# Where a norm scale is multiplied in, and which engines split weights into a rounded part and a rest, in a two-layer encoder step

## The chip, the cores and the metric

The program runs on one core of a Trainium2 chip. The metric is the device time of one execution in microseconds (us). The time before is the median of three timed runs. The core has five engines that run their own instruction lists in order and wait for each other through semaphores: TensorE (PE in the profile, its weight loads PEld), VectorE (DVE), ScalarE (ACT), GpSimd (POOL), and SyncE (SP), which issues the DMAs.

## The reference, cut to what matters

Each of two layers normalises its input, projects it to 13 groups of columns, runs four kinds of attention on them, and projects back. The parts that the change touches:

```python
def rms(x, g):
    xf = x.astype(jnp.float32)
    y = xf * lax.rsqrt(jnp.mean(xf * xf, -1, keepdims=True) + EPS)
    return (y * g.astype(jnp.float32)).astype(x.dtype)

xn = rms(x, lp['norm_g'])                       # (2048 + 64 rows) x 1024
aq, ak, av, ag, bcq, ... = split_in(xn @ lp['w_in'])
k, v = jnp.split(rms(mem, lp['m_norm_g']) @ lp['w_mem_kv'], 2, axis=-1)
y = rms(heads(y, N_OUT_HEADS), lp['out_g'].reshape(N_OUT_HEADS, HEAD_DIM))
y = y.reshape(x.shape[:2] + (MIX_WIDTH,)) * jax.nn.silu(gates)
return x + y @ lp['w_out']
```

In all three projections a gain `g` per input feature stands between the normalised activations and the weights. Since `(x * g) @ W` and `x @ (g * W)` (row k of W scaled by g of feature k) are the same product, the gain can be multiplied into either side. The factor per row of `rms`, the rsqrt, is applied at the end, when a product leaves PSUM.

## The kernel before, in words

Projections run in a three-product form: both sides are split into a part rounded to the matmul's type (`h`, float32r) and the rest (`l`), and a product is `xh*wh + xh*wl + xl*wh`. In the code `xh`, `xl` are the transposed activations of one tile of 128 rows (8 k tiles of 128 features each) and `wh` is one buffer that holds the rounded weights and, behind them, the rest.

The rows are split into three blocks (6, 6 and 5 tiles; the last tile is the 64 sample rows). A *job* is one projection of one block: `i` is the input projection (13 *chunks* of at most 256 output columns), `o` the output projection (4 chunks), `m` the memory's keys and values (2 chunks, 2 tiles). The jobs run in the order `i00 m00 i01 i02 o00 m10 o01 i10 i11 o02 i12 o10 o11 o12` (layer, block), 106 chunks in all. Within a chunk the loop runs over the tiles of the block, and within a tile over the 8 k tiles.

- `prep` makes a tile's `xh` and `xl`, in two halves of four k tiles: TensorE transposes (L259), ScalarE copies the half from PSUM with rounding (L266, 512 columns), VectorE subtracts (`sub_r`, L136, 512 columns). This happens once per tile and job, one tile ahead of the products in the first chunk of a job, or during the last chunk of the job before.
- `weights` makes one chunk's weights: four DMAs of two k tiles each into `raw`, then for each k tile GpSimd multiplies by the gain column and rounds (L304, `gc[:, k:k+1]`), and VectorE computes `raw * gain - h` (L305). There are 8 buffers `wh`, one per k tile, which is one chunk's worth: the k tile of the next chunk can only be written when the last tile of this chunk has used the old one. So all of a chunk's splitting happens around the *boundary* between two chunks, and the next chunk's first tile follows at once.
- `p_stream` runs the jobs and interleaves `feed` (the next weights) with the products (L402, L403, L405; for the narrow chunk of 160 columns L400 and L405). `pp` (PSUM, two buffers) is evicted by ScalarE (`ev`, L437).
- `attention` runs beside it: scores, a maximum or a scan on VectorE, exponentials or sigmoids on ScalarE, transposes, the split `ph` (L903 on ScalarE, L136 on VectorE), and the product with the values (L925). In group C (`Stick`) VectorE scans (L1110) and GpSimd multiplies (L1113).

The program's text gives the order in which work is generated; a scheduler then fixes the order of the instructions on every engine from its own model of durations.

Of the kernel before, what the change touches and what calls it, by code (L numbers as in the profile page):

```python
# [7 lines left out]
F32 = mybir.dt.float32  # L8
F32R = mybir.dt.float32r
BF16 = mybir.dt.bfloat16  # L10
ACTF = mybir.ActivationFunctionType
# [53 lines left out]
def hybrid_step(  # L65
# [12 lines left out]
    SAMP = NT  # L78
# [157 lines left out]
        if left[tag] == 0:  # L236
            done.add(tag)

    def prep(load, norm, acts, t, split):

        xs = []
        for q in range(2):
            xs.append(pj.tile([128, 512], F32, tag="xin", name="xin", bufs=2))
            load(xs[q], q)
        yield 0
        xh = pj.tile([128, 8, 128], F32R, tag="xh", name="xh", bufs=MAXB)
        xl = pj.tile([128, 8, 128], F32R, tag="xl", name="xl", bufs=MAXB)
        st = None
        if norm:
            st = pj.tile([128, 4], F32, tag="xst", name="xst", bufs=MAXB + 1)  # L250
        acts[t] = (xh, xl, st)
        for q in range(2):
            x = xs[q]
            if norm:
                A.activation(out=xl[:, q * 4:q * 4 + 4].rearrange("p a b -> p (a b)"), in_=x, func=ACTF.Square,
                             accum_out=st[:, q:q + 1])
            pt = ps_st.tile([128, 4, 128], F32, name="ptx")
            for k in range(4):
                T.transpose(pt[:, k, :], x[:, k * 128:(k + 1) * 128], ident)  # L259
            ks = slice(q * 4, q * 4 + 4)  # L260
            if t == SAMP and split:
                A.copy(out=xl[:, ks], in_=pt)
                copy_r(xh[:, ks, 0:64], xl[:, ks, 0:64].bitcast(F32))
                sub_r(xh[:, ks, 64:128], pt[:, :, 64:128], xl[:, ks, 64:128])
            else:
                A.copy(out=xh[:, ks], in_=pt)  # L266
                sub_r(xl[:, ks], pt, xh[:, ks])
            yield 1024
        if norm:
            V.tensor_tensor(out=st[:, 2:3], in0=st[:, 0:1], in1=st[:, 1:2], op=ALU.add)  # L270
            V.tensor_scalar(out=st[:, 2:3], in0=st[:, 2:3], scalar1=1.0 / 1024, scalar2=EPS,
                            op0=ALU.mult, op1=ALU.add)
            rpow(st[:, 3:4], st[:, 2:3], 1)
# [22 lines left out]

    def weights(job, c0, w, out):

        gc = job.gcols()

        def split(raw, k):
            hl = pj.tile([128, 512], F32R, tag="wh", name="wh", bufs=8)
            h, lo = hl[:, 0:w], hl[:, w:2 * w]
            G.tensor_scalar(out=h, in0=raw, scalar1=gc[:, k:k + 1], scalar2=1.0, op0=ALU.mult, op1=ALU.mult)  # L304
            V.scalar_tensor_tensor(out=lo, in0=raw, scalar=gc[:, k:k + 1],  # L305
                                   in1=h.bitcast(F32), op0=ALU.mult, op1=ALU.subtract)
            out.append((hl[:, 0:2 * w], h, lo))

        n = 2
        src = job.wsrc[:, 8 * c0:8 * (c0 + w)].rearrange("p (k c) -> p k c", k=8)  # L310
        raws = []
        for k in range(0, 8, n):
# [2 lines left out]
            raws.append(raw)  # L315
            yield 0
            if k > 0:
                for i in range(n):
                    split(raws[-2][:, i, 0:w], k - n + i)
                    yield 0  # L320
        for i in range(n):
            if i:
                yield 0
            split(raws[-1][:, i, 0:w], 8 - n + i)

    def p_stream(jobs):
        chunks = [(j,) + c for j in jobs for c in j.chunks]
# [32 lines left out]
        def start_prep(j, t):  # L360

            if (j, t) not in ready:
                ready.add((j, t))
                begin(j)
                preps[j, t] = prep(j.loader(t), j.norm, j.acts, t, j.folds(t))
                next(preps[j, t])

        def prep_tile(j, t):
# [1202 lines left out]
```

## Time and profile before

| | |
|---|---|
| median of three runs | 3382.83 us (3377.99 to 3388.35) |
| profiled execution | 3392.03 us, span 3390.2 us |
[...]
| PE busy | 94% of the span, 24486 matmuls |
| DVE busy | 80%, 7976 instructions |
| ACT busy | 57%, 5336 instructions |
| POOL busy | 47%, 2353 instructions |

The three pointwise engines are not equally loaded: VectorE is busy for four fifths of the span, ScalarE and GpSimd for about half of it. A matmul of 256 columns is shown at about 290 ns although the next one starts long before its end, so idle time of PE is shorter than what a wait costs. A row of the waits says which engine waited for whose instruction, for how long in all, how many times, and how long the longest took.

### The profile page before, as it was taken

Reading aid. Unit: us, or ns where it says so; the run is one execution under the profiler, and the core shown is the slowest. Engines: PE = TensorE matmul, PEld = TensorE weight load, DVE = VectorE, ACT = ScalarE, POOL = GpSimd, SP = SyncE. Lnnn points to the kernel's source line nnn. Section 1 sums busy time; section 2 is a strip of 40 time slices with the busy share of each in tenths; the row PEclk is TensorE's granted clock in tenths of the full one; section 3 lists DMA queues with packets and bytes.
Section 4 is the critical chain, followed back from the end, with each engine's and each line's share of the span. In section 5 each row is a group of like instructions: output and inputs, shape, how many; then the busy total and the mean of one; then the engine's idle time right before and its main releaser. Section 6 shows DMA issues by size and latency. Waiting matters only on the chain. (4 is left out here: it accounts for less than half of the span.)

```text
span 3390.2 us, 75857 instructions
## 1 busy us (share of the span) xinstructions
PE 3177.9 (94%) x24486; PEld 3029.8 (89%) x24486; DVE 2728.9 (80%) x7976; ACT 1939.0 (57%) x5336; POOL 1598.4 (47%) x2353
## 2 busy tenths in 40 slices
PE   8999899899999998999999899988999999999898
PEld 7899899789999988999999788978898998888898
DVE  5686777999788789887778977899878888776994
ACT  4455655567665555566556665656646566654651
POOL 4564455666344256542434635477424454112563
PEclk9999999999999998999999999999999999999999
DMA  6555776435656656565566567634455766556534
GB/s 198 168 147 165 205 203 191 131 101 155 172 155 192 194 165 166 141 191 154 145 186 193 146 177 209 194 111 118 140 142 160 207 193 192 151 149 179 153 110 147
DMA packets 576123, 558.95 MB, mean 165 GB/s; under 512 B 70960, under 2 KB 478000, under 8 KB 575728
## 3 DMA queue, kind: packets, MB, share of 16 engines
q1 hardware_dynamic: 575728, 554.10, 58.3%
q8 instruction: 196, 3.21, 0.4%
q14 instruction: 199, 1.63, 0.2%
HBM read 378.21 MB, written 173.75 MB: 163 GB/s over the span
## 5 line engine op out<-in xcount | busy, mean ns | idle before, releaser
L403 PE MATMUL pp<-wh,xh 128*128 128x256 f32 x4416 | 1268.4, 291 | 33.6 <-DVE wh L305 32.3
L402 PE MATMUL pp<-wh,xh 128*128 128x256 f32 x4416 | 1259.8, 290 | 21.9 <-ACT ev L437 14.4
L405 PE MATMUL pp<-wh,xl 128*128 128x256 f32 (+1 forms) x4416 | 1250.5, 285 | 0.6 <-DVE xl L136 0.4
L403 PEld LDWEIGHTS pp<-wh,xh 128*128 128x128 f32 x4416 | 839.9, 191 | 64.0 <-DVE wh L305 51.3
L402 PEld LDWEIGHTS pp<-wh,xh 128*128 128x128 f32 x4416 | 837.5, 191 | 39.2 <-ACT ev L437 18.5
L405 PEld LDWEIGHTS pp<-wh,xl 128*128 128x128 f32 x4416 | 845.1, 192 | 9.3 <-DVE xl L136 0.8
L304 POOL TENSOR_SCALAR wh<-raw,gc 128x256 fp32r<-128x256 f32 (+1 forms) x848 | 500.1, 604 | 301.6 <-PE pp L405 146.3
L925 PE MATMUL ot<-ph,kv 128*128 128x256 f32 (+1 forms) x3104 | 591.8, 294 | 34.3 <-DVE ph L136 18.8
L903 ACT CAST ph<-pt 128x512 fp32r<-128x512 f32 (+2 forms) x840 | 451.0, 551 | 259.6 <-PE pt L900 231.0
L136 DVE TENSOR_TENSOR ph<-pt,ph 128x512 fp32r<-128x512 f32 (+2 forms) x840 | 525.9, 634 | 68.7 <-ACT ph L903 64.8
L900 PE MATMUL pt<-identr,s 128*128 128x128 f32 x3056 | 509.7, 277 | 25.2 <-POOL s L1113 8.0
L925 PEld LDWEIGHTS ot<-ph,kv 128*128 128x128 f32 x3104 | 458.7, 191 | 56.5 <-DVE ph L136 28.0
L1113 POOL TENSOR_TENSOR s<-s,r 128x512 f32<-128x512 f32 (+3 forms) x328 | 359.6, 1102 | 311.4 <-DVE r L1110 136.9
L305 DVE SCALAR_TENSOR_TENSOR wh<-raw,gc,wh 128x256 fp32r<-128x256 f32 (+1 forms) x848 | 472.5, 582 | 25.0 <-POOL wh L304 22.9
L1110 DVE TENSOR_TENSOR_SCAN r<-cc,r 128x512 f32<-128x512 f32 (+3 forms) x328 | 406.5, 1250 | 15.9 <-ACT cc L1093 14.4
L139 POOL TENSOR_TENSOR st<-st,mhalf 128x4 f32<-128x4 f32 (+1 forms) x312 | 283.3, 913 | 270.9 <-DVE st L463 240.4
L855 PE MATMUL ps<-kv,qbuf 128*128 128x512 f32 (+3 forms) x1024 | 376.7, 371 | 25.7 <-DVE ph L136 5.4
L900 PEld LDWEIGHTS pt<-identr,s 128*128 128x128 f32 x3056 | 361.8, 141 | 43.6 <-POOL s L1113 12.4
L856 PE MATMUL ps<-kv,qbuf 128*128 128x512 f32 (+3 forms) x1024 | 351.1, 345 | 0.0
L437 ACT ACTIVATE ev<-pp,xst 128x256 f32<-128x256 f32 (+1 forms) x424 | 199.9, 473 | 161.7 <-PE pp L405 118.4
L1093 ACT ACTIVATE cc<-ps 128x512 f32<-128x512 f32 (+3 forms) x328 | 178.2, 544 | 192.5 <-DVE ps L1090 153.7
L1051 ACT ACTIVATE s<-s,nm 128x512 f32<-128x512 f32 (+3 forms) x328 | 212.6, 651 | 107.2 <-DVE nm L1043 74.3
(171 smaller groups left out, 5128.9 us busy)
## 6 DMA issues: line engine op xcount, KB each, us to landing
raw<-in_w_in SPq DMA_DIRECT2D x288, 256.0 KB, 3.5
kv<-kvC SPq DMA_DIRECT2D x128, 256.0 KB, 4.3
kv<-kvB SPq DMA_DIRECT2D x128, 256.0 KB, 4.4
kv<-kvA SPq DMA_DIRECT2D x96, 256.0 KB, 4.5
raw<-in_w_out SPq DMA_DIRECT2D x96, 256.0 KB, 3.4
y<-y SPq DMA_DIRECT2D x136, 128.0 KB, 2.5
xin<-y SPq DMA_DIRECT2D x64, 256.0 KB, 3.5
qC<-kt SPq DMA_DIRECT2D x34, 256.0 KB, 3.0
```

The lines of the kernel that those rows point to most:

```text
L136: (eng or V).tensor_tensor(out=dst, in0=src, in1=hi.bitcast(F32), op=ALU.subtract)
L304: G.tensor_scalar(out=h, in0=raw, scalar1=gc[:, k:k + 1], scalar2=1.0, op0=ALU.mult, op1=ALU.mult)
L305: V.scalar_tensor_tensor(out=lo, in0=raw, scalar=gc[:, k:k + 1], in1=h.bitcast(F32), op0=ALU.mult, op1=ALU.subtract)
L402: T.matmul(pp, lhsT=xh[:, k], rhs=wh, start=(k == 0), stop=False)
L403: T.matmul(pp, lhsT=xh[:, k], rhs=wl, start=False, stop=end)
L405: T.matmul(pp[:, 0:w], lhsT=xl[:, k], rhs=wh, start=False, stop=(k == 7))
L855: T.matmul(ps[:, 0:w], lhsT=q[:, 0, qs], rhs=kt[:, c0:c0 + w], start=True, stop=False)
L900: T.transpose(pt[:, (u + x) * 128:(u + x + 1) * 128], self.p_of(i, j), ident)
L903: A.copy(out=ph[:, 0:w], in_=pt[:, 0:w])
L925: T.matmul(ot[:, e * lo, il[0]:il[0] + n], lhsT=p["vt"](j), rhs=phl[:, e, u * 128:(u + n) * 128], start=start and e == 0, stop=stop and e ...
L1110: V.tensor_tensor_scan(r[:, 0:w][:, ::-1], cc[:, 0:w][:, ::-1], cc[:, 0:w][:, ::-1], r[:, w:w + 1], ALU.mult, ALU.min)
L1113: G.tensor_tensor(out=s[:, 0:w], in0=s[:, 0:w], in1=r[:, 1:w + 1], op=ALU.mult)
```

## The change

The gain is no longer multiplied into the weights. `prep` takes the gain columns `gc` and multiplies them into the transposed activations while it rounds them: four ScalarE instructions of 128 columns with a scale per partition in place of one copy of 512, and four VectorE instructions (multiply, subtract) of 128 columns in place of one subtraction of 512. `weights` then only has to round and to subtract: ScalarE copies two k tiles in one instruction, GpSimd subtracts two k tiles in one instruction, and VectorE has no part in it. There are 4 buffers `wh` of two k tiles in place of 8 of one.

```diff
-    def prep(load, norm, acts, t, split):
+    def prep(load, norm, acts, t, split, gc):
...
-            if t == SAMP and split:
-                A.copy(out=xl[:, ks], in_=pt)
+            fold = t == SAMP and split
+            hi, cs = (xl, slice(64, 128)) if fold else (xh, slice(0, 128))
+            lo = xh if fold else xl
+
+            for k in range(4):
+                kk = q * 4 + k
+                A.activation(out=hi[:, kk], in_=pt[:, k], func=ACTF.Copy, scale=gc[:, kk:kk + 1])
+            for k in range(4):
+                kk = q * 4 + k
+                V.scalar_tensor_tensor(out=lo[:, kk, cs], in0=pt[:, k, cs], scalar=gc[:, kk:kk + 1],
+                                       in1=hi[:, kk, cs].bitcast(F32), op0=ALU.mult, op1=ALU.subtract)
+            if fold:
                 copy_r(xh[:, ks, 0:64], xl[:, ks, 0:64].bitcast(F32))
-                sub_r(xh[:, ks, 64:128], pt[:, :, 64:128], xl[:, ks, 64:128])
-            else:
-                A.copy(out=xh[:, ks], in_=pt)
-                sub_r(xl[:, ks], pt, xh[:, ks])
...
-        def split(raw, k):
-            hl = pj.tile([128, 512], F32R, tag="wh", name="wh", bufs=8)
-            h, lo = hl[:, 0:w], hl[:, w:2 * w]
-            G.tensor_scalar(out=h, in0=raw, scalar1=gc[:, k:k + 1], scalar2=1.0, op0=ALU.mult, op1=ALU.mult)
-            V.scalar_tensor_tensor(out=lo, in0=raw, scalar=gc[:, k:k + 1],
-                                   in1=h.bitcast(F32), op0=ALU.mult, op1=ALU.subtract)
-            out.append((hl[:, 0:2 * w], h, lo))
+        def split(raw):
+            hl = pj.tile([128, n, 512], F32R, tag="wh", name="wh", bufs=4)
+            h, lo = hl[:, :, 0:w], hl[:, :, w:2 * w]
+            A.copy(out=h, in_=raw)
+            G.tensor_tensor(out=lo, in0=raw, in1=h.bitcast(F32), op=ALU.subtract)
+            for i in range(n):
+                out.append((hl[:, i, 0:2 * w], h[:, i], lo[:, i]))
```

VectorE's order at the boundary ahead of the chunk `ak` of job `i01` (us 659 to 675 of the trace; L305 is the weights' rest, L1110 a scan, `ph` the attention's split, `kt` and `nrm` are keys of the projection), before:

```order
L1110 SCALAR_TENSOR_TENSOR r<-cc,r 128x512
L305 SCALAR_TENSOR_TENSOR wh<-raw,gc,wh 128x256
L474 TENSOR_TENSOR nrm<-ev,st 128x256
L305 SCALAR_TENSOR_TENSOR wh<-raw,gc,wh 128x256
L136 TENSOR_TENSOR ph<-pt,ph 128x512
L501 SCALAR_TENSOR_TENSOR kt<-ptk,qg,kt 128x256
L1109 COPY r<-r 128x1
L462 TENSOR_REDUCE st<-sq 128x4
L136 TENSOR_TENSOR ph<-pt,ph 128x512
L1110 SCALAR_TENSOR_TENSOR r<-cc,r 128x512
L463 TENSOR_SCALAR st<-st 128x4
L305 SCALAR_TENSOR_TENSOR wh<-raw,gc,wh 128x256 x2
```

The same place on VectorE now (lines behind the edit have a number one higher):

```order
L1111 SCALAR_TENSOR_TENSOR r<-cc,r 128x512
L463 TENSOR_REDUCE st<-sq 128x4
L1110 COPY r<-r 128x1
L475 TENSOR_TENSOR nrm<-ev,st 128x256
L464 TENSOR_SCALAR st<-st 128x4
L136 TENSOR_TENSOR ph<-pt,ph 128x512
L502 SCALAR_TENSOR_TENSOR kt<-ptk,qg,kt 128x256
L136 TENSOR_TENSOR ph<-pt,ph 128x512
L1111 SCALAR_TENSOR_TENSOR r<-cc,r 128x512 x2
```

The eight instructions of the weights are gone from VectorE's list, and the scans and splits of the attention follow each other.

ScalarE's order at the same boundary (`cc` and `s` are the sigmoids of group C, `ev` the eviction of a product), before:

```order
L437 ACTIVATE ev<-pp,xst 128x256
L903 CAST ph<-pt 128x512
L500 ACTIVATE kt<-ptk,qg 128x256
L460 ACTIVATE sq<-ev 128x256
L903 CAST ph<-pt 128x512
L1093 ACTIVATE cc<-ps 128x512
L1094 ACTIVATE s<-ps 128x512
L1093 ACTIVATE cc<-ps 128x512
L1094 ACTIVATE s<-ps 128x512
L437 ACTIVATE ev<-pp,xst 128x256
```

The same place on ScalarE now, from the square of the same eviction on:

```order
L461 ACTIVATE sq<-ev 128x256
L310 CAST wh<-raw 128x2x256
L904 CAST ph<-pt 128x512
L501 ACTIVATE kt<-ptk,qg 128x256
L904 CAST ph<-pt 128x512
L1094 ACTIVATE cc<-ps 128x512
L1095 ACTIVATE s<-ps 128x512
L310 CAST wh<-raw 128x2x256
L1094 ACTIVATE cc<-ps 128x512
L1095 ACTIVATE s<-ps 128x512
L310 CAST wh<-raw 128x2x256 x2
L438 ACTIVATE ev<-pp,xst 128x256
```

Four copies of weights now stand between the attention's splits and sigmoids; the first of them is ahead of a split `ph` and of a key `kt`.

GpSimd's order there, before (`mst` and `st` are row factors, L1113 the product of group C, L1107 and L1108 set the start of a scan):

```order
L304 TENSOR_SCALAR wh<-raw,gc 128x256 x2
L1113 TENSOR_TENSOR s<-s,r 128x384
L1113 TENSOR_TENSOR s<-s,r 128x512
L304 TENSOR_SCALAR wh<-raw,gc 128x256 x3
L1107 MEMSET r 128x1
L304 TENSOR_SCALAR wh<-raw,gc 128x256 x3
L1113 TENSOR_TENSOR s<-s,r 128x512
```

And now:

```order
L311 TENSOR_TENSOR wh<-raw,wh 128x2x256
L139 TENSOR_TENSOR st<-st,mhalf 128x4
L1108 MEMSET r 128x1
L311 TENSOR_TENSOR wh<-raw,wh 128x2x256
L1114 TENSOR_TENSOR s<-s,r 128x512 x2
L311 TENSOR_TENSOR wh<-raw,wh 128x2x256 x2
L1108 MEMSET r 128x1
```

Eight instructions of one k tile became four of two, with as much other work between them.

## Rows read from the trace of the kernel before

**Rows 1.** The page: busy us (share of the span) and instructions of each engine.

```profile
PE 3177.9 (94%) x24486; PEld 3029.8 (89%) x24486; DVE 2728.9 (80%) x7976; ACT 1939.0 (57%) x5336; POOL 1598.4 (47%) x2353
```

**Rows 2.** The waits of PE: engine, line, waited for; us in total, times, longest.

```profile
PE pp L403 <- DVE wh L305: 32.3, 49, 2.1
PE ot L925 <- DVE ph L136: 18.8, 27, 1.9
PE pp L402 <- ACT ev L437: 14.4, 13, 4.1
...
PE ptk L494 <- ACT ev L437: 8.1, 6, 3.5
...
PE ps L855 <- DVE xl L136: 5.1, 4, 3.3
PE pt L900 <- ACT s L999: 5.1, 11, 1.3
PE ot L925 <- ACT ph L903: 5.1, 7, 1.3
```

**Rows 3.** The waits of the weight loads, the longest one.

```profile
PEld pp L403 <- DVE wh L305: 51.3, 85, 2.3
```

**Rows 4.** Four boundaries: stretch, length, then busy us of PE, PEld, DVE, ACT, POOL.

```profile
659.30:674.90 15.60, 12.20 (x92) 10.99 (x90) 15.50 (x24) 7.86 (x18) 11.04 (x15) 1.00 0.56 156
1295.50:1312.90 17.40, 14.18 (x91) 12.76 (x89) 17.24 (x26) 5.88 (x13) 14.24 (x17) 0.90 0.40 105
1863.70:1877.60 13.90, 10.50 (x80) 9.66 (x79) 13.83 (x28) 6.49 (x19) 11.10 (x17) 1.00 0.41 113
2260.80:2274.30 13.50, 10.91 (x77) 9.71 (x75) 13.47 (x22) 7.17 (x18) 13.38 (x15) 0.93 0.69 192
```

**Rows 5.** POOL's groups by form: count, busy us, mean ns of one, idle before.

```profile
L304 POOL TENSOR_SCALAR wh<-raw,gc 128x256 fp32r<-128x256 f32 x800 | 479.3, 614 | 285.7 <-PE pp L405 146.1 <-PE pp L403 88.1 <-issue 37.2
L1113 POOL TENSOR_TENSOR s<-s,r 128x512 f32<-128x512 f32 x224 | 279.4, 1253 | 189.3 <-DVE r L1110 68.2 <-ACT s L1094 27.0 <-ACT ph L903 12.6
```

**Rows 6.** DVE's groups by form.

```profile
L305 DVE SCALAR_TENSOR_TENSOR wh<-raw,gc,wh 128x256 fp32r<-128x256 f32 x800 | 452.5, 591 | 24.4 <-POOL wh L304 22.9 <-DMA qr<-qr 1.0 <-POOL r L1107 0.3
...
L136 DVE TENSOR_TENSOR xl<-ptx,xh 128x512 fp32r<-128x512 f32 x136 | 92.2, 682 | 16.7 <-ACT xh L266 16.3
...
L501 DVE SCALAR_TENSOR_TENSOR kt<-ptk,qg,kt 128x256 fp32r<-128x256 f32 x102 | 48.3, 473 | 3.7 <-ACT kt L500 3.6
...
L305 DVE SCALAR_TENSOR_TENSOR wh<-raw,gc,wh 128x160 fp32r<-128x160 f32 x48 | 19.9, 443 | 0.6 <-POOL r L1107 0.6
...
L429 DVE SCALAR_TENSOR_TENSOR ev<-pp,xst,ev 128x160 f32<-128x160 f32 x32 | 12.1, 378 | 3.3 <-ACT ev L437 3.0
```

**Rows 7.** ACT's groups by form.

```profile
L437 ACT ACTIVATE ev<-pp,xst 128x256 f32<-128x256 f32 x392 | 187.2, 479 | 158.1 <-PE pp L405 115.5 <-DVE nrm L474 8.9 <-issue 7.7
...
L931 ACT COPY os<-ot 128x256 f32<-128x256 f32 x352 | 131.3, 373 | 55.8 <-PE ot L925 38.4 <-PE ot L921 16.5
L266 ACT CAST xh<-ptx 128x512 fp32r<-128x512 f32 x136 | 79.4, 595 | 33.0 <-PE ptx L259 32.2
...
L946 ACT COPY opark<-ob 128x128 f32<-128x128 f32 x256 | 69.9, 273 | 27.5 <-PE ob L941 27.1
...
L255 ACT ACTIVATE xl<-xin 128x512 fp32r<-128x512 f32 x76 | 48.0, 635 | 51.7 <-DMA xin<-in_x_prompt 24.6 <-DMA xin<-x 21.0 <-DMA xin<-in_x_sample 3.7
```

**Rows 8.** Waits of POOL for a free weight buffer.

```profile
POOL wh L304 <- PE pp L405: 146.3, 39, 28.5
...
POOL wh L304 <- PE pp L403: 88.1, 25, 18.2
```

**Rows 9.** Line 304 alone: count, shortest, median and longest ns.

```profile
L304 POOL TENSOR_SCALAR wh<-raw,gc x848: 392/595/1487, 7.6 to 3372.1; 128x256 fp32r<-128x256 f32 x159, 128x160 fp32r<-128x160 f32 x11
```

**Rows 10.** A stretch of the first job, in which no attention runs; columns as in the boundaries.

```profile
26.00:32.00 6.00, 4.20 (x31) 3.67 (x30) 4.85 (x25) 4.00 (x14) 4.13 (x11) 1.00 0.64 179
```

More of the change, by code (lines that the diff above doesn't have):

```diff
@@ L297, in weights @@
     def weights(job, c0, w, out):
-        gc = job.gcols()
-        def split(raw, k):
-            hl = pj.tile([128, 512], F32R, tag="wh", name="wh", bufs=8)
-            h, lo = hl[:, 0:w], hl[:, w:2 * w]
-            G.tensor_scalar(out=h, in0=raw, scalar1=gc[:, k:k + 1], scalar2=1.0, op0=ALU.mult, op1=ALU.mult)
-            V.scalar_tensor_tensor(out=lo, in0=raw, scalar=gc[:, k:k + 1],
-                                   in1=h.bitcast(F32), op0=ALU.mult, op1=ALU.subtract)
-            out.append((hl[:, 0:2 * w], h, lo))
-        n = 2
+        n = 2
+        def split(raw):
[5 more added lines that the diff above has]
+                out.append((hl[:, i, 0:2 * w], h[:, i], lo[:, i]))
         src = job.wsrc[:, 8 * c0:8 * (c0 + w)].rearrange("p (k c) -> p k c", k=8)
@@ L317, in weights @@
             if k > 0:
[L318 to L322, printed above, removed]
+                split(raws[-2][:, :, 0:w])
                 yield 0
-            split(raws[-1][:, i, 0:w], 8 - n + i)
+        split(raws[-1][:, :, 0:w])
     def p_stream(jobs):
@@ L364, in start_prep @@
                 begin(j)
-                preps[j, t] = prep(j.loader(t), j.norm, j.acts, t, j.folds(t))
+                preps[j, t] = prep(j.loader(t), j.norm, j.acts, t, j.folds(t), j.gcols())
                 next(preps[j, t])
```

## Prediction

> **What bounds the kernel now.** I read the page first, then the waits of PE, then the groups of each pointwise engine, then windows at the chunk boundaries.
>
> The page [rows 1] says that TensorE is the bound: PE is busy for 3177.9 of 3390.2 us, and the change neither adds nor removes a matmul. So all that can be gained or lost lies in PE's idle 212.3 us, and in what a wait costs beyond its idle time. Of the pointwise engines VectorE is the fullest with 80%, ScalarE has 57%, GpSimd 47%.
>
> The waits of PE [rows 2] say whom it waits for. The largest row is the one that the change removes: PE waits 49 times, 32.3 us in all, for the rest of the weights, which VectorE computes on line 305. The weight loads, which run ahead of the matmuls, show the same wait at 51.3 us in 85 times [rows 3]. As a matmul is drawn longer than its distance to the next, I take 32.3 as the lower and 51.3 as the upper price of this wait today.
>
> The windows [rows 4] say why it waits. The four stretches are boundaries between chunks where PE waits longest. VectorE is busy for 15.50 of 15.60 us, 17.24 of 17.40, 13.83 of 13.90 and 13.47 of 13.50: it is full. ScalarE is busy for 34% to 53% of the same stretches. GpSimd has 71%, 82%, 80% and, in the fourth, 13.38 of 13.50 us. So at a boundary the splitting is held up by VectorE's queue, in one of the four by GpSimd as much.
>
> **The change part by part.**
>
> *Weights on VectorE, removed.* 848 instructions, 452.5 + 19.9 = 472.4 us busy [rows 6]; per chunk 8 x 0.591 = 4.7 us.
>
> *Weights on GpSimd, replaced.* Before: 8 x 0.614 = 4.9 us per chunk [rows 5]. Now four subtractions of 128 x 512 with both inputs in SBUF. The row of that form is L1113: 1.253 us [rows 5], so 4 x 1.253 = 5.0 us. GpSimd's share of a boundary stays as it is.
> Line 304 takes between 392 and 1487 ns [rows 9], with a median of 595, although nearly all have one form: something stretches it. [...]
>
> *Weights on ScalarE, added.* 424 copies of two k tiles. The nearest row with an SBUF source and 512 columns is L255 with 635 ns [rows 7]; 400 x 0.635 = 254 us, and for the 24 narrow ones at most 24 x 0.635 = 15 us: some 265 us, 4 x 0.635 = 2.5 us per chunk.
>
> *Activations.* There are 136 halves of a tile (and eight of the sample tile, counted alike): 144. On ScalarE one copy of 595 ns becomes four of 128 columns with a scale per partition. A plain copy of 128 columns takes 273 ns (L946); the scale costs 479 - 373 = 106 ns (L437 against L931, 256 columns each) [rows 7]; so 379 ns. 576 x 0.379 - 144 x 0.595 = 218 - 86 = +132 us. On VectorE one subtraction of 682 ns becomes four of the kind of L501 and L429: 473 ns at 256 columns, 378 at 160 [rows 6], which is 0.99 ns per column and 346 ns at 128. 576 x 0.346 - 144 x 0.682 = 199 - 98 = +101 us.
>
> Busy time then: VectorE 2728.9 - 472.4 + 101 = 2358 us (70%), ScalarE 1939.0 + 265 + 132 = 2336 us (69%), GpSimd as before. VectorE and ScalarE are then equally full. What of this reaches PE:
>
> *1. PE's wait for the weights.* In the four windows I take 4.7 us from VectorE, add 2.5 to ScalarE and leave GpSimd. VectorE then has 10.8, 12.5, 9.1 and 8.8 us of work, ScalarE 10.4, 8.4, 9.0 and 9.7, GpSimd 11.0, 14.2, 11.1 and 13.4. The fullest engine is GpSimd each time; the boundary could shrink by 4.6, 3.2, 2.8 and 0.1 us. PE was idle there for 3.4, 3.2, 3.4 and 2.6 us, so 3.4 + 3.2 + 2.8 + 0.1 = 9.5 of 12.6 us go, 75%. What is late next is the subtraction on GpSimd. 75% of 32.3 to 51.3 us is 24 to 38 us; as the idle time of PE itself is the harder number I take -24. Bounds: -51 below, if all of it goes, and a loss above. The first rest of a chunk used to be ready 0.614 + 0.591 = 1.2 us after its buffer was free; now it takes 0.635 + 1.253 = 1.9 us, and if PE paid these 0.7 us at every one of the 106 boundaries it would be +74. I stay near the lower end, since PE shows a wait at fewer than half of the boundaries (49), and since the last pair of a chunk comes no later than now.
>
> *2. PE's other waits for VectorE.* The two rows shown are 18.8 + 5.1 = 23.9 us [rows 2]. VectorE's load falls by 371 of 2729 us, 14%; in that proportion -3 us. Bounds 0 and -24.
>
> *3. PE's waits for ScalarE.* The four rows are 14.4 + 8.1 + 5.1 + 5.1 = 32.7 us [rows 2]. ScalarE's load grows by 397 of 1939 us, 20%; in that proportion +7 us. The upper bound: the copy waits for a free buffer, at the head of a queue that also holds evictions, splits and sigmoids. GpSimd waits for this today, 39 times for 146.3 us and 25 times for 88.1 us [rows 8], and it has less behind it that PE needs. If in every one of the 106 boundaries PE paid for one copy, it would be 106 x 0.635 = +67 us. Below nothing it cannot be, since nothing is taken from ScalarE. Between ends this far apart I stay near the row of the waits, because ScalarE has 43% of its time free over the span and about half of it free in the windows.
>
> *4. The activations' longer way.* The half is ready later: four copies take 1.5 us where one took 0.6. Beside attention, and one tile ahead, this has cover. In the first job there is no attention: from 26 to 32 us PE is busy for 4.20 of 6.00 us, ScalarE for 4.00, VectorE for 4.85 [rows 10]. A tile's preparation adds 2 x (4 x 0.379 - 0.595) = 1.8 us to ScalarE, six tiles 11 us, if ScalarE were full; it has a third free, so I take +3. Bounds 0 and +11.
>
> Sum: -24 - 3 + 7 + 3 = -17 us. Against the profiled execution's own 3392.0 us that makes 3375. The median of the three runs shown is 9.2 us below the profiled one; at the median it makes 3382.8 - 17 = 3366 us.
>
> **The rivals.**
>
> *No change.* GpSimd takes VectorE's place as the engine for which the weights wait. For it: its work per chunk is the same 5 us, in pieces of twice the length, and the fourth window has it full already. Against it: the other three windows, with 18% to 29% free. The wait then stays near its 32.3 us with another name, and the small terms cancel: 3375 to 3390, say 3382 us. [...]
>
> *Slower: ScalarE's queue.* The copies wait at the head of ScalarE's list for PE to release a weight buffer, while the splits `ph` and the evictions `ev` behind them, which PE needs within the same boundary, are ready. For it: the new order has the first copy directly ahead of a `ph` and a `kt`, and the two longest waits of PE for `ev` are 4.1 and 3.5 us [rows 2], so ScalarE is late at times even now. Against it: the copies stand where the scheduler's model has the buffer free, and PE's order passes the release before it needs what stands behind. At the full price of one copy per boundary it is +67, with terms 1, 2 and 4: -24 - 3 + 67 + 3 = +43, 3426 us; at half of it 3392. It decides from the point where PE's waits for ScalarE grow by more than 27 us, that is by more than 0.25 us per boundary.
>
> *Faster, more than that.* VectorE's relief reaches all waits that end in its full stretches, and GpSimd's pieces come out shorter. Terms 1 and 2 at their ends, -51 - 24, with +7 and +3: -65, 3318 us. For it: weight loads show 85 late weights, not 49. Against it: PE waits for `ph` 27 times [rows 2], at a quarter as many places as there are boundaries, and no row shown ties them to the weights.
>
> **How the numbers follow.** Forecast, -10 to -40 us: 0.44. More than that: 0.12. No change: 0.21. Slower: 0.23. A measurement of this kernel can tell about 0.3%, 10 us, from no change. The forecast and the faster rival give 0.56 for faster, the second 0.21 for the same, the third 0.23 for slower. The time is the forecast's, 3366. Its own range is 3343 to 3376. The range that takes the rivals in reaches down to 3322, near the end of the faster rival, and up to 3408, the middle of the slower one.
>
> **What would show it.** Right: in the waits of PE the row for the weights' rest is under half of 32.3 us, named GpSimd instead of VectorE; VectorE near 70% and ScalarE near 69% of the span; the copies near 0.63 us, the subtractions between 1.1 and 1.25 us; the four stretches shorter, with GpSimd fullest. Wrong in term 1: a row of PE for the weights of 30 us or more. Wrong in term 3: rows of PE for `ev`, `ph` and `s` from ScalarE that together exceed 60 us, or ScalarE idle for a weight buffer while its next split is ready. Wrong in term 4: a first job that ends more than 5 us later. Since every engine's order is made anew, waits at single places will come and go without any of this being their cause; a difference under 10 us says nothing on the steps.

## The result: slower by 28 us, and the profile after

The changed kernel takes 3410.06 us (median of six runs, 3399.42 to 3414.99); the kernel before took 3381.94 us on the same chip (six runs, 3377.66 to 3388.35). The ratio is 1.0078, 95% interval 1.0058 to 1.0098. Forecast were 3366 us; the result has the other sign and lies 2 us above the upper end of the range.

The page of the changed kernel, span and busy times, to set beside [rows 1]:

```profile
span 3413.2 us, 75701 instructions
PE 3172.7 (93%) x24486; PEld 3028.5 (89%) x24486; DVE 2575.6 (75%) x7560; ACT 2219.5 (65%) x6192; POOL 1656.8 (49%) x1929
```

PE does the same work (3172.7 us against 3177.9) and is idle for 3413.2 - 3172.7 = 240.5 us instead of 212.3. So the loss between the profiled runs is idle time of PE. VectorE should have fallen to 2358 us; it is at 2575.6.

The granted clock of TensorE, as a share of the full one, has a small part in the medians. Its mean is 0.985 over the six runs of the changed kernel and 0.987 over the runs of the kernel before that stand beside the experiments. From run to run of one kernel, over all kernels here, the time falls by about 1.7 us per 0.001 of granted clock; by this estimate some 4 of the 28 us go with the clock.

The waits of PE in the changed kernel (engine, line, waited for; us in total, times, longest), which answer to [rows 2]:

```profile
PE ot L926 <- DVE ph L136: 28.2, 26, 3.6
...
PE pp L406 <- DVE xl L270: 11.6, 16, 2.4
PE pt L901 <- DVE mx L981: 11.2, 7, 3.8
...
PE pp L403 <- ACT ev L438: 9.8, 9, 2.3
PE pp L404 <- POOL wh L311: 9.4, 15, 1.4
PE ps L856 <- DVE ph L136: 8.1, 8, 2.4
...
PE pt L901 <- ACT s L1000: 7.6, 13, 1.8
PE ptk L495 <- ACT ev L438: 7.3, 4, 3.8
PE pt L901 <- DVE ph L136: 6.0, 5, 2.4
...
PE pp L401 <- POOL wh L311: 3.1, 2, 1.8
...
PE pp L403 <- ACT wh L310: 2.0, 3, 1.1
...
PE ot L926 <- ACT ph L904: 1.3, 2, 0.9
```

Most of the wait that the change was to remove is gone: 32.3 us for the weights' rest became 9.4 + 3.1 us, and 2.0 us for the rounded part. The weight loads say the same; this row answers to [rows 3], where it was 51.3 us:

```profile
PEld pp L404 <- POOL wh L311: 13.0, 16, 1.6
```

ScalarE's four rows sum to 9.8 + 7.3 + 7.6 + 1.3 = 26.0 us against 32.7. What grew are VectorE's rows: `ph`, 18.8 before, has 28.2; the maximum `mx`, 0.6 us on this row before, 11.2; `xl`, 8.3 us over all its rows before, 12.5. Adding up the idle time ahead of every matmul by its releaser (gaps over 150 ns) gives for the profiled runs, before and after: weights 34.7 and 14.6 us, everything else from VectorE 75.7 and 116.0, other work of GpSimd 8.3 and 15.3, DMAs 39.3 and 44.3, other work of ScalarE 42.4 and 37.4. So -20 us as meant, and +40 us from a VectorE that has less to do; some 4 of these 40 are `xl`, whose making the change itself cut into four pieces.

Why VectorE is late can be read in its groups by form. First the added operations of the changed kernel on GpSimd and ScalarE, then five groups of VectorE that the change doesn't touch (count, busy us, mean ns of one, idle before):

```profile
L311 POOL TENSOR_TENSOR wh<-raw,wh 128x512 fp32r<-128x512 f32 x400 | 539.7, 1370 | 287.2 <-ACT wh L310 268.2 <-issue 5.6 <-DMA raw<-in_w_mem 4.7
L310 ACT CAST wh<-raw 128x512 fp32r<-128x512 f32 x400 | 238.9, 636 | 48.1 <-PE pp L404 25.8 <-PE pp L406 11.7 <-issue 6.4
L267 ACT ACTIVATE xh<-ptx,gc 128x128 fp32r<-128x128 f32 x544 | 156.7, 398 | 40.2 <-PE ptx L259 35.4 <-PE pp L404 4.2
L270 DVE SCALAR_TENSOR_TENSOR xl<-ptx,gc,xh 128x128 fp32r<-128x128 f32 x544 | 152.5, 341 | 29.9 <-ACT xh L267 29.5
...
L136 DVE TENSOR_TENSOR ph<-pt,ph 128x512 fp32r<-128x512 f32 x616 | 415.9, 682 | 70.9 <-ACT ph L904 67.1
L1111 DVE TENSOR_TENSOR_SCAN r<-cc,r 128x512 f32<-128x512 f32 x224 | 349.8, 1574 | 7.3 <-ACT cc L1094 5.6 <-POOL r L1108 0.9
L475 DVE TENSOR_TENSOR nrm<-ev,st 128x256 f32<-128x256 f32 x106 | 71.3, 672 | 27.0 <-POOL st L139 18.7 <-PE ptk L495 3.2 <-POOL r L1108 2.5
L464 DVE TENSOR_SCALAR st<-st 128x4 f32<-128x4 f32 x210 | 56.2, 269 | 1.3
L1047 DVE TENSOR_TENSOR f<-nm 128x2 f32<-128x2 f32 x96 | 26.8, 279 | 1.8
```

The same five groups in the kernel before:

```profile
L136 DVE TENSOR_TENSOR ph<-pt,ph 128x512 fp32r<-128x512 f32 x616 | 415.9, 682 | 58.0 <-ACT ph L903 54.6
L1110 DVE TENSOR_TENSOR_SCAN r<-cc,r 128x512 f32<-128x512 f32 x224 | 327.1, 1470 | 6.8 <-ACT cc L1093 6.4 <-issue 0.2
L474 DVE TENSOR_TENSOR nrm<-ev,st 128x256 f32<-128x256 f32 x106 | 58.2, 549 | 17.2 <-POOL st L139 10.0 <-DMA o_akp<-nrm 4.8 <-PE ptk L494 1.4
L463 DVE TENSOR_SCALAR st<-st 128x4 f32<-128x4 f32 x210 | 40.9, 197 | 0.9
L1046 DVE TENSOR_TENSOR f<-nm 128x2 f32<-128x2 f32 x96 | 15.9, 166 | 1.4
```

One copy, one scaled piece of activations and one piece of `xl` last about what was forecast (636, 398 and 341 ns, against 635, 379 and 346). The pieces overlap, though: 544 of 398 ns keep ScalarE busy for 156.7 us and not for 217, and 544 of 341 ns keep VectorE busy for 152.5 us and not for 186. The split `ph`, which reads PSUM, is unchanged to the nanosecond. But the same instructions from SBUF to SBUF are longer: 197 to 269 ns, 166 to 279, 549 to 672, and the scan 1470 to 1574.

One of them in the timeline of the changed kernel (start us, us, engine; idle before it and who ended it, in brackets). `nm` negates the maxima that the exponentials `s` need:

```profile
2201.52 1.29 POOL L311 TENSOR_TENSOR wh<-raw,wh 128x512 fp32r<-128x512 f32 x1
...
2201.55 1.28 DVE L989 TENSOR_SCALAR nm<-mx 128x2 f32<-128x2 f32 x1
...
2202.75 0.41 DVE L1355 TENSOR_TENSOR y<-opark,mst 128x256 f32<-128x256 f32 x1
...
2202.87 0.51 ACT L1000 ACTIVATE s<-s,nm 128x256 f32<-128x256 f32 x1 [1.46 <-DVE nm L989]
```

Two elements per partition take 1.28 us instead of 0.16, the median of this line: `nm` starts 30 ns after GpSimd's subtraction and ends with it, and ScalarE waits 1.46 us for it. All instances of this line in the changed kernel (shortest, median and longest ns):

```profile
L989 DVE TENSOR_SCALAR nm<-mx x144: 136/161/1281, 408.5 to 3133.0; 128x2 f32<-128x2 f32 x128, 128x1 f32<-128x1 f32 x16
```

and in the kernel before:

```profile
L988 DVE TENSOR_SCALAR nm<-mx x144: 132/159/368, 403.7 to 3110.0; 128x2 f32<-128x2 f32 x128, 128x1 f32<-128x1 f32 x16
```

In the other three orders of the kernel before, which the experiments bring, the longest is 652 to 697 ns.

To size it, I took for every form of VectorE instruction the shorter quarter's duration as its own length, and summed what instructions lasted beyond it, by the GpSimd instruction that they overlapped most. Under L311 that is some 191 us of VectorE time, nearly all of it in 242 instructions that are over 0.2 us too long. This *held time* is used below.

### The profile page after: what moved, and what is told of

Its sections match the earlier page's. It is cut to its first block, busy times and chain, and to the rows that moved or that the text cites. A ratio compares the mean times of both kernels' runs of the same rounds, so it can differ in the third digit from the quotient of the medians.

```text
span 3413.2 us, 75701 instructions
## 1 busy us (share of the span) xinstructions
PE 3172.7 (93%) x24486; PEld 3028.5 (89%) x24486; DVE 2575.6 (75%) x7560; ACT 2219.5 (65%) x6192; POOL 1656.8 (49%) x1929
## 4 chain that ended last, share of the span: by engine, by line
PE 32%; DVE 12%; DMA 9%; issue 4%; ACT 3%; POOL 3%; SPq 2%; POOLq 0%; DVEq 0%; ACTq 0%
PE pp L403 5%; PE pp L404 5%; PE pp L406 5%; PE ot L926 4%; PE pt L901 4%; DVE r L1111 3%; PE ps L856 2%; PE ps L857 2%; DVE ph L136 2%; PE ps L859 1%; PE ob L942 1%; DMA y<-y 1%; POOL wh L311 1%; POOL s L1114 1%; DMA kv<-kvC 1%
## 5 line engine op out<-in xcount | busy, mean ns | idle before, releaser
L311 POOL TENSOR_TENSOR wh<-raw,wh 128x512 fp32r<-128x512 f32 (+1 forms) x424 | 562.9, 1348 | 302.9 <-ACT wh L310 283.8
L926 PE MATMUL ot<-ph,kv 128*128 128x256 f32 (+1 forms) x3104 | 582.4, 294 | 37.3 <-DVE ph L136 28.2
L901 PE MATMUL pt<-identr,s 128*128 128x128 f32 x3056 | 509.1, 277 | 48.1 <-DVE mx L981 11.2
L926 PEld LDWEIGHTS ot<-ph,kv 128*128 128x128 f32 x3104 | 455.3, 192 | 58.8 <-DVE ph L136 37.4
L1114 POOL TENSOR_TENSOR s<-s,r 128x512 f32<-128x512 f32 (+3 forms) x328 | 371.6, 1142 | 275.6 <-DVE r L1111 115.2
L1111 DVE TENSOR_TENSOR_SCAN r<-cc,r 128x512 f32<-128x512 f32 (+3 forms) x328 | 442.5, 1361 | 15.0 <-ACT cc L1094 12.5
L310 ACT CAST wh<-raw 128x512 fp32r<-128x512 f32 (+1 forms) x424 | 249.9, 628 | 49.8 <-PE pp L404 25.8
```

The costliest lines, as they stand in the source:

```text
L311: G.tensor_tensor(out=lo, in0=raw, in1=h.bitcast(F32), op=ALU.subtract)
L901: T.transpose(pt[:, (u + x) * 128:(u + x + 1) * 128], self.p_of(i, j), ident)
L926: T.matmul(ot[:, e * lo, il[0]:il[0] + n], lhsT=p["vt"](j), rhs=phl[:, e, u * 128:(u + n) * 128], start=start and e == 0, stop=stop and e ...
L1111: V.tensor_tensor_scan(r[:, 0:w][:, ::-1], cc[:, 0:w][:, ::-1], cc[:, 0:w][:, ::-1], r[:, w:w + 1], ALU.mult, ALU.min)
L1114: G.tensor_tensor(out=s[:, 0:w], in0=s[:, 0:w], in1=r[:, 1:w + 1], op=ALU.mult)
```

## Experiments

Three theories stood at first. *Hold*: GpSimd's subtractions keep VectorE's small instructions open. *ScalarE's queue*: the copies of weights delay what stands behind them. *Preparation*: the activations come later in four pieces. All ratios are to the kernel before, run beside each kernel on the same chip.

**Preparation alone** (`e1_prep_alone`). The activations as in the change; the weights are split as before, by GpSimd and VectorE, with a factor of one.

```diff
-            G.tensor_scalar(out=h, in0=raw, scalar1=gc[:, k:k + 1], scalar2=1.0, op0=ALU.mult, op1=ALU.mult)
-            V.scalar_tensor_tensor(out=lo, in0=raw, scalar=gc[:, k:k + 1],
+            G.tensor_scalar(out=h, in0=raw, scalar1=1.0, scalar2=1.0, op0=ALU.mult, op1=ALU.mult)
+            V.scalar_tensor_tensor(out=lo, in0=raw, scalar=1.0,
```

> The gain on the activations as in the change; the weights split as before, one k tile at a time, GpSimd rounding and VectorE subtracting, with a factor of one in place of the gain. Theory of the hold (while GpSimd runs a subtraction with two inputs, some 1.3 us, VectorE's instructions on SBUF stay open): no such subtraction here, so 3380 to 3392 us, and the longest negated maximum (nm, 128x2) back under 0.5 us from 1.28. Theory of the preparation (four pieces per half are late): 3395 to 3412. Theory of ScalarE's queue (the copies of weights): near before, 3380 to 3392.

3386.96 us, 1.0008 (0.9995 to 1.002). In this one order the longer way of the activations costs nothing that can be measured, although VectorE is at its fullest here (the longest `nm`, 693 ns, is over the 0.5 us expected, but no longer than in other orders of the kernel before):

```profile
PE 3173.3 (94%) x24486; PEld 3018.3 (89%) x24486; DVE 2737.5 (81%) x8408; ACT 2011.2 (59%) x5768; POOL 1512.6 (45%) x2353
```

**Weights alone** (`e2_weights_alone`). The weights as in the change, the preparation as before; the gains are left out altogether.

```diff
-                A.activation(out=hi[:, kk], in_=pt[:, k], func=ACTF.Copy, scale=gc[:, kk:kk + 1])
...
+                A.copy(out=xh[:, ks], in_=pt)
+                sub_r(xl[:, ks], pt, xh[:, ks])
```

> The weights as in the change (ScalarE rounds, GpSimd subtracts, two k tiles each); the activations prepared as before in two instructions per half. The norm gains are left out altogether. Theory of the hold and theory of ScalarE's queue: slow as the changed kernel, 3400 to 3412 us, with nm up to 1.3 us long. Theory of the preparation: as before, 3378 to 3388.

3375.73 us, 0.998 (0.9968 to 0.9993). The theories of the hold and of ScalarE's queue missed: the held time is there in full (188 us), and yet this kernel is no slower than before. In the profile the trade is there all the same: PE's idle time for weights is 14.2 us, for other work of VectorE 95.8, against 34.7 and 75.7 before; here the two nearly cancel, and PE's idle time in all is 217.7 us against 212.3. In the one order that each had, either part alone costs nothing and both together 28 us. As the scheduler lays every engine's order anew for each kernel, the next question was what an order by itself is worth.

**Other orders** (`c1_order`, `c3_order_m55`, `c5_order_a141` of before; `c2_order_after`, `c4_order_after_m55`, `c6_order_after_a141` of the changed kernel). One of the numbers by which the program interleaves attention with the projections is moved by some 1%; instructions and their counts stay, the order changes everywhere.

```diff
-WEIGHT = {"A": 1.4, "B": 0.72, "C": 0.85, "M": 0.56}
+WEIGHT = {"A": 1.4, "B": 0.72, "C": 0.85, "M": 0.57}
```

> The kernel before with one number of the interleaving changed (the weight of group M 0.57 in place of 0.56), the same instructions. It measures how much a new order alone moves the time. If the cases so far are told apart by mechanisms, it stays within 0.3% of before (3373 to 3393 us); if orders alone move it by 0.5% or more, differences of that size say nothing.

> The changed kernel with the same number changed. Theory of the hold: the loss belongs to the instructions, not to this one order, so 3398 to 3420 us, and VectorE's small instructions are again up to 1.3 us long. Theory that the changed kernel had an unlucky order: 3370 to 3392 us, like the run with the weights' part alone.

> The kernel before with the weight of group M at 0.55, a third order of the same instructions. With the two orders so far (3382 and 3362 us) as a sample, 3350 to 3395 us. It is paired with the changed kernel in the same setting.

> The changed kernel with the weight of group M at 0.55. Theory that the change costs in any order (hold on VectorE, some 15 to 30 us): slower than the kernel before in the same setting by 10 to 35 us, as it was in the two settings so far (by 28 and 14). Theory that the order alone made the loss: as fast as its partner within 10 us, or faster.

> The kernel before with the weight of group A at 1.41, a fourth order of the same instructions: 3350 to 3395 us. Partner of the changed kernel in the same setting.

> The changed kernel with the weight of group A at 1.41. Theory that the change costs in any order: slower than its partner by 10 to 35 us. Theory that the order alone made the loss: within 10 us of its partner, or faster.

Times with their ratios, and PE's idle time in the profiled run by releaser, in us (weights / other work of VectorE / other work of GpSimd):

| order | before | changed | idle before | idle changed |
|---|---|---|---|---|
| M 0.56 | 3381.94, 1 | 3410.06, 1.0078 (1.0058 to 1.0098) | 34.7 / 75.7 / 8.3 | 14.6 / 116.0 / 15.3 |
| M 0.57 | 3361.64, 0.994 (0.9924 to 0.9957) | 3375.31, 0.9986 (0.9976 to 0.9995) | 23.8 / 82.0 / 7.7 | 23.2 / 79.7 / 13.2 |
| M 0.55 | 3397.14, 1.005 (1.0032 to 1.0067) | 3396.6, 1.0046 (1.0034 to 1.0058) | 31.3 / 90.5 / 3.9 | 18.6 / 104.8 / 14.5 |
| A 1.41 | 3376.16, 0.9972 (0.9956 to 0.9988) | 3394.69, 1.0033 (1.0015 to 1.0051) | 26.3 / 74.7 / 7.8 | 13.5 / 93.2 / 22.0 |
| mean | 0.9991 | 1.0036 | 29.0 / 80.7 / 6.9 | 17.5 / 98.4 / 16.3 |

An order alone moves the kernel before by -0.6% to +0.5%, 36 us from end to end, more than any term of the prediction. Pair by pair the change costs 0.78, 0.46, -0.04 and 0.61 points, in the mean 0.45 or 15 us; four pairs with that scatter leave the mean uncertain by 0.56 points (95%), so in the times a loss over orders is likely and not proved. By that mean about half of the 28 us belongs to this order. Against the expectations: `c1_order` and `c3_order_m55` fell outside theirs, `c2_order_after` and `c4_order_after_m55` came out as an unlucky order would have it, `c6_order_after_a141` as a cost in any order would.

PE's idle time in the profiled runs, span less busy time, is clearer. It grows in all four pairs, by 28.2, 9.4, 13.1 and 20.8 us, in the mean by 18 us, uncertain by 13 (95%). The times scatter more because PE's busy time differs too, from 3157 to 3184 us in these eight runs with the same matmuls; the runs don't show why. In the mean PE waits less for weights (-11.5 us; at M 0.57 hardly less) and longer for VectorE's other work (+18; at M 0.57 it is 2 us shorter, though that pair has a loss too) and for GpSimd's (+9, in every pair). VectorE is busy for 2563 to 2576 us each time, and the longest `nm` is between 1281 and 1321 ns.

**One k tile per subtraction** (`e5_one_k`). The changed kernel with the same subtractions in pieces of half the length; nothing else.

```diff
-            G.tensor_tensor(out=lo, in0=raw, in1=h.bitcast(F32), op=ALU.subtract)
             for i in range(n):
+                G.tensor_tensor(out=lo[:, i], in0=raw[:, i], in1=h[:, i].bitcast(F32), op=ALU.subtract)
```

> The changed kernel with GpSimd's subtraction in two instructions of one k tile each (848 of some 0.73 us); ScalarE rounds two k tiles as in the change. GpSimd's time per chunk grows by 8 x 0.73 - 4 x 1.37 = 0.4 us. Theory that the length of one hold counts (one VectorE instruction is stuck for up to 1.3 us): 3375 to 3395 us, nm at most 0.75 us. Theory that the total time with two inputs open counts: 3400 to 3415 us.

3377.14 us, 0.9994 (0.9979 to 1.0008): 33 us less than the changed kernel in the same order (0.84 points of the ratios, 28 us), though GpSimd is now busier. That is less than the 36 us that lie between orders of one kernel, and this kernel ran in one order only. Its group, and `nm` in this kernel:

```profile
L312 POOL TENSOR_TENSOR wh<-raw,wh 128x256 fp32r<-128x256 f32 x800 | 623.3, 809 | 264.5 <-ACT wh L310 196.3 <-issue 66.4 <-POOL wh L312 0.9
```

```profile
L989 DVE TENSOR_SCALAR nm<-mx x144: 135/164/785, 406.5 to 3090.4; 128x2 f32<-128x2 f32 x128, 128x1 f32<-128x1 f32 x16
```

The held time falls to 128 us. If a VectorE instruction meets a GpSimd instruction at a random moment and is held to its end, held time goes with busy time times length: 191 x (623.3 / 539.7) x (809 / 1370) = 130. PE's idle time for other work of VectorE falls with it, from 116.0 to 77.4 us. The longest `nm` is 785 ns, a little over the expected 0.75 us.

**One input instead of two** (`e3_one_input`; in other orders `d4_one_input_m57`, `d5_one_input_m55`; with the preparation as before `e6_one_input_old_prep`). GpSimd's subtraction becomes two instructions that read `raw` alone.

```diff
-            G.tensor_tensor(out=lo, in0=raw, in1=h.bitcast(F32), op=ALU.subtract)
+            for _ in range(2):
+                G.tensor_scalar(out=lo, in0=raw, scalar1=0.0, scalar2=1.0, op0=ALU.mult, op1=ALU.mult)
```

> The changed kernel, but GpSimd's subtraction of a pair of k tiles is replaced by two instructions of the same shape with one input each, some 2 x 0.7 us, so that GpSimd works as long; the rest of the weights is left out (zeros). Theory of the hold: VectorE's unchanged instructions shrink back (nm at most 0.5 us, VectorE under 72% busy) and the time falls to 3360 to 3388 us. Theory that GpSimd is simply too slow, or ScalarE's queue too full: 3400 to 3415, since both have the same work.

> The weights' part alone (activations prepared as before, no norm gains at all) with GpSimd's subtraction replaced by two instructions with one input each (the weights' rest left out, zeros). Theory of the hold: it is faster than the run with the weights' part alone (3376 us) by as much as the same swap gave in the full change, some 55 us: 3320 to 3340. If the hold costs only together with the four-piece preparation: 3360 to 3376 us.

> The run with one-input instructions on GpSimd (two per pair of k tiles, the weights' rest left out, zeros) at 0.57 for group M. Theory of the hold: 20 to 55 us faster than the changed kernel in this setting (3375), so 3320 to 3355 us. Theory that the order made the 55 us of the first such run: 3360 to 3390.

> The same at 0.55 for group M (weights' rest left out). Theory of the hold: 20 to 55 us faster than the changed kernel in this setting (3397), so 3342 to 3377 us. Theory of the order: 3380 to 3410.

3355.63 us, 0.9912 (0.9893 to 0.9931); at M 0.57 3345.28, 0.9898 (0.9876 to 0.9921); at M 0.55 3363.17, 0.9946 (0.993 to 0.9963). Against the changed kernel in the same order that is -54, -30 and -33 us. With the old preparation 3348.92, 0.9912 (0.9897 to 0.9928), 27 us below the weights alone, half of the 55 us that the theory of the hold expected there. The first run is faster than that theory's range, and its `nm` (633 ns) and VectorE's share (74%) stay above what was expected. The page and `nm` of the first, and GpSimd's group:

```profile
PE 3153.0 (94%) x24486; PEld 3015.0 (90%) x24486; DVE 2471.4 (74%) x7560; ACT 2221.2 (66%) x6192; POOL 1640.3 (49%) x2353
```

```profile
L990 DVE TENSOR_SCALAR nm<-mx x144: 114/160/633, 406.3 to 3077.6; 128x2 f32<-128x2 f32 x128, 128x1 f32<-128x1 f32 x16
```

```profile
L312 POOL TENSOR_SCALAR wh<-raw 128x512 fp32r<-128x512 f32 x800 | 532.0, 687 | 266.3 <-PE pp L405 115.3 <-PE pp L407 75.5 <-ACT s L1001 31.5
```

GpSimd is as busy as in the change (1640.3 us, 1656.8), and ScalarE too; VectorE has 104 us less with the same instructions. The held time is 90 us; by length and busy time, as above, it would be 191 x (532.0 / 539.7) x (687 / 1370) = 94. So two inputs aren't needed to hold VectorE, and for these two instructions the held time goes with the length of GpSimd's piece. Two things more differ. PE's busy time is 20 us lower than in the change (3153.0 us, 3172.7), so that of the 59 us between the two profiled spans 39 are PE's idle time; the rest of the weights is zeros here, and whether that has a part in the 20 us, no run shows. And these instructions don't read `h`, so GpSimd no longer waits for ScalarE's copy (268.2 us of idle time in the change). What share of the 54 us that has, this run can't tell; `e5_one_k`, which keeps that wait, has 33 us from the pieces alone, in one order.

**VectorE subtracts** (`e4_vector_subtracts`; in other orders `d1_vector_m57`, `d2_vector_m55`). The changed kernel with GpSimd taken out of the weights; the computation is complete.

```diff
-            G.tensor_tensor(out=lo, in0=raw, in1=h.bitcast(F32), op=ALU.subtract)
+            sub_r(lo, raw, h)
```

> The changed kernel with the subtraction of the weights on VectorE, two k tiles per instruction; ScalarE rounds as in the change, GpSimd has no part in the weights. Theory of the hold: VectorE gets 424 x 0.68 = 290 us of work but loses some 190 us of holding, so about 78% busy, and 3350 to 3388 us. Theory of ScalarE's queue: the copies and the four-piece preparation are all still there, 3400 us or more. Theory of the preparation: 3395 or more.

> The changed kernel with the weights subtracted on VectorE, at 0.57 for group M. Theory of the hold: no two-input instruction on GpSimd for the weights, so 10 to 45 us faster than the changed kernel in this setting (3375): 3330 to 3365 us, and faster than the kernel before in this setting (3362) or equal. Theory of ScalarE's queue or of the preparation: no gain, 3365 to 3385.

> The same at 0.55 for group M. Theory of the hold: 3352 to 3387 us against 3397 of the changed kernel in this setting. Theory of ScalarE's queue or of the preparation: 3385 to 3405.

3358.78 us, 0.9928 (0.9912 to 0.9944); at M 0.57 3355.34, 0.9932 (0.9913 to 0.9951); at M 0.55 3363.95, 0.9961 (0.9949 to 0.9973). This beats the changed kernel in each order, by 51, 20 and 33 us, as the theory of the hold had it, and the kernel before in two of three clearly (0.72, 0.08 and 0.89 points). PE's idle time for other work of VectorE is 79.2, 78.5 and 87.0 us, against 116.0, 79.7 and 104.8 in the change in the same orders. Page and waits of the first:

```profile
PE 3161.9 (94%) x24486; PEld 3018.2 (90%) x24486; DVE 2635.7 (79%) x7984; ACT 2217.4 (66%) x6192; POOL 1131.0 (34%) x1505
```

```profile
PE ot L926 <- DVE ph L136: 25.2, 35, 1.8
...
PE pp L404 <- DVE wh L136: 14.4, 23, 1.7
```

VectorE carries 294 us of subtractions of the full form more than in the change, and its busy time is only 60 us higher: some 191 of the other 234 us are what L311 held in the change. The row for `ph` stays long in total (25.2 us), with more and shorter waits. All of PE's idle time for weights is 16.0, 16.8 and 27.0 us in the three orders, in the mean 19.9 against 18.8 in the change: the wait stays as short in the mean although VectorE subtracts again, so VectorE's absence isn't needed to shorten it.

In the runs of the last three headings, those with the old preparation left aside, the mean granted clock is 0.003 to 0.006 higher than in the changed kernel of the same order. By the estimate above, 4 to 11 us of each gain go with the clock.

**ScalarE rounds, the rest as before** (`f1_scalar_rounds_before`). The kernel before; ScalarE multiplies and rounds each k tile in place of GpSimd. The computation is complete, the gain stays on the weights.

```diff
-            G.tensor_scalar(out=h, in0=raw, scalar1=gc[:, k:k + 1], scalar2=1.0, op0=ALU.mult, op1=ALU.mult)
+            A.activation(out=h, in_=raw, func=ACTF.Copy, scale=gc[:, k:k + 1])
```

> The kernel before (gain on the weights, one k tile at a time, VectorE computing the rest) with ScalarE multiplying and rounding in place of GpSimd: 848 instructions of some 0.48 us on ScalarE, none on GpSimd. Theory of the hold: GpSimd's one-input instructions on the weights hold VectorE only a little, so little is won, 3365 to 3385 us. Theory that any work of GpSimd beside VectorE's costs: as fast as the run that subtracts pairs on VectorE, 3350 to 3364 us, and then the gain's move has no part in that run's time.

3362.79 us, 0.9938 (0.9914 to 0.9962). The wait for the weights:

```profile
PE pp L403 <- DVE wh L305: 23.0, 39, 1.9
```

This is inconclusive. The time is in the range of the theory that any work of GpSimd beside VectorE's costs, and as good as that of `e4_vector_subtracts` within the intervals, without moving the gain; but `c1_order` has the same ratio, 0.994, and nearly the same wait (22.0 us in this row) by its order alone, and this kernel ran in one order only.

## Why the prediction was wrong, point by point

*What bounds the kernel.* Right: PE's idle time grew by 28.2 us and its busy time fell by 5.2.

*Weights' wait, -24 us.* Right in this order: 34.7 to 14.6 us, -20. Over four orders it is -11.5, since the wait of before is itself a matter of the order (23.8 to 34.7 us). The wait's new name is GpSimd's, as forecast, so this term's own sign of being right came true while the time went the other way.

*Subtraction at 1.253 us.* Near, 0.12 us too short: 1.370 us in the mean for the full form. GpSimd's busy time is 1656.8 us where 1598.4 were taken over.

*VectorE falls to 2358 us, its other waits by 3 us.* This step failed. It says "GpSimd as before" and subtracts durations, as though an instruction lasted the same beside any neighbour. VectorE came to 2575.6 us, 218 more: 191 us are held under L311 in this count (before, 72 us were held under L304, a good part of it on line 305 itself, which is gone), and the waits for it grew by 40 us where 3 were to go. With GpSimd out of the weights (`e4_vector_subtracts`) those waits are back at 79.2 us, near the 75.7 of before. The term also started from two rows, 23.9 us, where all waits for VectorE other than for weights are 75.7. And a share of busy time was the wrong measure for this term. The scans L1111 have the largest single part of the held time, some 34 us; much of the rest falls on short instructions in the middle of the attention's chain (`nm`, `st`, `f`), delayed by up to 1.1 us each, and with them what follows, as the exponential in the timeline that waits for `nm`.

The rows of before held the warning. GpSimd's product on L1113 is of the kind that was added, 128 x 512 with two inputs. In the trace of before the held time under it is 92.7 us for 279.4 us of its busy time [rows 5], 0.33 us per us. The 400 subtractions at 1.253 us would by that hold VectorE for 0.33 x 501 = 166 us, an estimate; without the part on line 305, which goes (23 of the 92.7 us), some 124 us. The prediction took from L1113's row only the length of the subtraction itself. In the trace of the changed kernel `nm` is open for 1.28 us beside a subtraction of 1.29; other GpSimd instructions hold next to nothing (none of 145 under line 139 of the kernel before), as the last section shows. By what means one engine holds the other, no run shows.

*ScalarE's waits, +7 us.* Wrong in sign, small in size: 32.7 to 26.0 us, with ScalarE 280 us busier. The load was over-sized, 397 us, since the four pieces of a half overlap. (By the prediction's own sum the slower rival breaks even at 24 us more of these waits; its 27 leaves out term 4.) The slower rival by ScalarE's queue, for which I gave 3426 us, has nearly the right time and the wrong cause.

*Activations' longer way, +3 us.* Right: the changed kernel is 3.2 us behind when PE has done 1200 matmuls (186.7 us against 183.5), PE's waits for `xl` grew by 4 us, and the preparation alone costs nothing measurable over the span in its one order. The rest of the loss builds up beside attention: 7.6 us after 2400 matmuls, 30 after 20400, 23 after 24000.

*The order.* The prediction said that a difference under 10 us says nothing on the steps, since waits at single places come and go. The orders show that this bound was too narrow: the same instructions in four orders lie between 3362 and 3397 us. The forecast of -17 us was smaller than that scatter, and the range should have been wider for it.

Settled by runs: the forecast relief of VectorE is not there, since GpSimd's subtractions hold many of its SBUF instructions until they end (120 of 129 of the short ones that the last section counts); without the subtraction on GpSimd the changed kernel is faster in each of three orders. Shown in one order only: with shorter pieces it is faster, and the preparation alone costs nothing. Open: how much of the 15 us in the mean is the hold and how much GpSimd's wait for ScalarE's copies; why the weights alone, with as much held time, lost nothing; and which instructions make one order worse than another.

## What to carry to other kernels

Price an instruction that is put on GpSimd also by its neighbour. In these runs its busy time, times its length, told how long VectorE's SBUF instructions stood, for a subtraction (128 us held where that gives 130) and for a multiplication by constants (90 where it gives 94); not for every kind (none of 145 under line 139), so look in a trace whether the kind at hand holds anything. Where the held instructions lie in a chain that TensorE waits for, another engine was better here (by 51, 20 and 33 us in three orders), and in the one order tried short pieces were better than one long piece (by 33 us). When a scheduler lays a new order for every edit, run the edit in several orders before believing half a per cent; one order is one draw.

## What the runs showed of the hardware

Which GpSimd instructions hold VectorE was unexpected, and so was which VectorE instructions are held. Counted are VectorE's instructions of at most 4 columns, SBUF to SBUF, that start under a GpSimd instruction and would by their own length end over 0.2 us ahead of it; held are those over 0.12 us too long. Of the kinds tensor-scalar, tensor-tensor and scalar-tensor-tensor, 120 of 129 are held under the subtraction L311, and end 20 ns (median) after it; under L1113 of before 29 of 30; under the one-input instruction of `e3_one_input` 101 of 111, with 8 ns. But under L304 of before, one input times a column of gains, only 8 of 59 are (12 to 17 of 67 or 68 in its other orders); and under the row factors of line 139 (the 128 x 4 ones about 1.07 us each) none of 145. VectorE's copies of one column, reciprocals and reads of its accumulators were not held: none of 132 under L311, none of 83 under L1113, none of 94 under the one-input instruction. VectorE's split `ph`, which reads PSUM, was not held at all (682 ns in the mean and at most 694 in both kernels).

So by these counts the mere presence of a GpSimd instruction isn't what holds. On L304 `e1_prep_alone` gives a hint: there GpSimd multiplies the same shape by the constant 1.0 in place of the column of gains, in shorter instructions (513 ns in the mean against 614), and 7 of 11 are held.

```profile
L308 POOL TENSOR_SCALAR wh<-raw 128x256 fp32r<-128x256 f32 x800 | 394.0, 513 | 250.0 <-PE pp L409 125.6 <-PE pp L407 94.9 <-issue 14.4
```

So it seems to be the column that goes with holding little. Why, the runs don't show, and eleven are few.
